# Block 0 of the gathered expert FFN: the weighted sum over rows of v as matmuls on PE, by token, in a PSUM bank that the recurrent mixer had

## The chip, the cores and the metric

One core of a Trainium2 chip runs one program. The metric is the time of one execution on the device in microseconds (us). An engine takes its instructions in the order of its own queue: PE is TensorE (PEld its weight loads), DVE is VectorE, ACT is ScalarE, POOL is GpSimd, and SP issues most of the DMAs.

## What is computed

A decoder block over 1,024 tokens of width 1,024: an RWKV-7 recurrent mixer and a differential attention side by side, merged by sigmoid gates, and then a PEER feed-forward. Of 16,384 experts each token chooses 128 (8 heads of 16); a row of `u_tab` gives each chosen expert its activation and a row of `v_tab`, weighted by it, is added up:

```
s = jnp.einsum('thcd,hcnd->thcn', q, sub_keys)
...
ids = (e1 * PK_NKEYS + e2).reshape(T, PK_HEADS * PK_TOPK)
gates = jax.nn.softmax(vals, axis=-1).reshape(T, PK_HEADS * PK_TOPK)
...
act = jnp.einsum('ced,cd->ce', u_tab[idc], xc)
act = jax.nn.gelu(act, approximate=False) * gc
return jnp.einsum('ce,ced->cd', act, v_tab[idc])
```

A final RMSNorm follows. All inputs and outputs are float32.

## The kernel before

The tokens go in two groups of 512 (`GROUPS`), and each group in blocks of 128 tokens. `mix` does a group's norm, input projections, four recurrent heads (`rwkv`), four attention heads (`attention`), the merge, the output projection (`w_out`) and the second norm; `pick` scores the keys. `choose` turns a block's scores into `ids` and `gate`. The four blocks of the first group go by **gathers** (`peer`): for each of the 128 choices j an indirect DMA from the POOL queue (`gather`) brings 128 rows of u, one for each token, into a tile `uv` of 128 x 1024 float32 (512 KB), and one DVE instruction multiplies it with the block's normed input `hb` and sums it into `act[:, j]` (L814). After the Gelu and the product with `gate` the same is done with v: DVE adds `v * act[:, j]` to `acc` (L821). All gathers share `NU` = 5 tiles `uv`. `finish` is the final norm and the store.

The four blocks of the second group go **dense** (`gates`, `ahead`, `dense`): all 128 stripes of 128 experts are computed by PE (`ua` is u against the tokens, `yk` and `yr` the weighted sums of v; six of the eight outputs are kept in PSUM over the whole loop, two are added to `accd` by DVE at L904).

`choose` of blocks 0 to 3 is called between the heads of the second group's mixer (`CHO`). The calls of `peer` stand last in the program, after `dense`. A planner orders each engine's queue: an instruction is put in when its inputs and a free buffer are there by the planner's own clock, the earlier in the program the more urgent. So the gathers and their DVE steps fill places that the planner found free in the second mixer, in `pick` and `gates`, and in `dense`.

PSUM has eight banks: two `zb` (projections, `q`, `ua`, `yr`), three `rb` (all that `rwkv` makes on PE), two `ab` and one `ob` (attention, transposes). The tag `ha` has two tiles of 128 x 1024, which hold `hb` and `acc` of the gathered blocks. `w_out` fills all eight banks at once (four token blocks by two column halves), and the additions to x (L668) come after the last matmul.

Names that the steps touch: `rbank` L62, `rwkv` L280 to L483 with its pairs of banks in `byfeat` (L421 to L430, read at L439, L442, L446, L450), `am` L331, `choose` L711, `gather` L790, `peer` L806, `dense` L861, the last loop L951.

Of the kernel before, what the change touches and what calls it, by code (L numbers as in the profile page):

```python
# [8 lines left out]
F32 = mybir.dt.float32  # L9
F32R = mybir.dt.float32r  # L10
BF = mybir.dt.bfloat16
I32 = mybir.dt.int32
U32 = mybir.dt.uint32
AF = mybir.ActivationFunctionType
OP = mybir.AluOpType
# [3 lines left out]
P = 128  # L19
D = 1024  # L20
T = 1024
# [8 lines left out]
NU = 5  # L30
ND = 4
NB = 5
NW = 3
# [14 lines left out]
def body(ctx: ExitStack, tc: tile.TileContext, ins, out, dbg=None):  # L48
# [13 lines left out]
    def rbank(name):  # L62
        return ps.tile([P, 512], F32, name=name, tag="rb", bufs=3)

# [179 lines left out]
    def mix(gi, t0, W):  # L244
# [409 lines left out]
        for a in range(TT):  # L654
            x1.append(t4("x1"))
            nc.sync.dma_start(x1[a], ins["x"][t0 + a * P:t0 + (a + 1) * P, :])
        banks = [f("xo") for f in (zbank, zbank, rbank, rbank, rbank, abank, abank, obank)[:2 * TT]]
        for k in range(8):
            w = [wsplit(ins["w_out"][k, i]) for i in range(2)]
            for a in range(TT):  # L660
                o = slice(a * P, (a + 1) * P)
                for i in range(2):
                    mm3(banks[2 * a + i], mh[k][:, o], ml[k][:, o], *w[i], k == 0, k == 7)
        for a in range(TT):
            rows = slice(t0 + a * P, t0 + (a + 1) * P)
            xs = [x1[a][:, c] for c in HALVES]
            for i in range(2):
                nc.vector.tensor_tensor(xs[i], xs[i], banks[2 * a + i], op=OP.add)  # L668
            nc.sync.dma_start(ins["x1s"][rows, :], x1[a])
            show("x1", x1[a], t0 // P + a)  # L670
            hn = normed(xs, nw)
            if t0 + a * P < T - ND * P:
                for i, c in enumerate(HALVES):
                    nc.sync.dma_start(ins["hfs"][rows, c], hn[i])
            to_cols(hn, a, fh, fl)
# [35 lines left out]
    def choose(v1, i1, bi, last):  # L711
# [75 lines left out]
        show("gate", gate, bi)  # L787
        return sl if last else (ids, gate)

# [15 lines left out]

    def peer(bi, ids, gate):  # L806

        rows = slice(bi * P, (bi + 1) * P)
        act = pp_.tile([P, P], F32, name="act", bufs=2)
        hb = pp_.tile([P, D], F32, name="hb", tag="ha", bufs=2)  # L810
        nc.sync.dma_start(hb, ins["hfs"][rows, :])
        for j in range(P):
            u = gather("u", ids, j)
            nc.vector.scalar_tensor_tensor(u, u, 1.0, hb, op0=OP.mult, op1=OP.mult, accum_out=act[:, j:j + 1])  # L814
        nc.scalar.activation(act, act, AF.Gelu)
        nc.vector.tensor_tensor(act, act, gate, op=OP.mult)
        acc = pp_.tile([P, D], F32, name="acc", tag="ha", bufs=2)
        nc.sync.dma_start(acc, ins["x1s"][rows, :])
        for j in range(P):
            v = gather("v", ids, j)  # L820
            nc.vector.scalar_tensor_tensor(acc, v, act[:, j:j + 1], acc, op0=OP.mult, op1=OP.add)  # L821
        finish(acc, rows, pp_, "uv", NU)

    def gates(sp, a, sl, eye8):
# [36 lines left out]
    def dense(t0, W, fh, fl):  # L861
# [7 lines left out]
        outs = [(a, 0) for a in range(TT)] + [(a, 1) for a in range(TT)][::-1]  # L869
        banks = (rbank, rbank, rbank, obank, abank, abank)  # L870
        kept = {o: f("yk") for o, f in zip(outs, banks)}
# [66 lines left out]
    if "nopeer" not in dbg:  # L938
        with tc.tile_pool(name="sp", bufs=1) as sp:
# [6 lines left out]
            for a, c in enumerate(late[o // P:]):  # L946
                gates(sp, a, choose(*c), eye8)
                ahead(sp, ND * P, fh, fl, range(a * NE // ND, (a + 1) * NE // ND))
            todo += [(c[2], *choose(*c)) for c in late[:o // P]]
        dense(t0 + o, ND * P, fh, fl)  # L950
        for t in todo:  # L951
            peer(*t)


def prepare(inputs):
# [31 lines left out]
    for b in (16, 32):  # L987
# [17 lines left out]

SCRATCH = {"x1s": (T, D), "hfs": (T, D), "k_s": (4, P, T), "v_s": (4, P, T),
           "y_s": (4, 8, P, 512), "g_s": (4, 16, P, 512),
# [20 lines left out]
```

## Time and profile before

| | us |
|---|---|
| median of 3 runs | 3537.24 |
| lowest and highest | 3536.96, 3545.42 |
| the profiled execution | 3524.41 |
| its span, first to last instruction | 3522.5 |

| engine | busy us | share of the span | instructions |
|---|---|---|---|
| PE | 3075.7 | 87% | 17382 |
| DVE | 2923.6 | 83% | 6546 |
| ACT | 1363.1 | 39% | 2506 |
| POOL | 1332.3 | 38% | 1036 |

The DMA engines are busy for most of the second half, and the mean rate is 255 GB/s. The span falls into stages that are best read apart: the first mixer and `pick` (0 to about 747 us, with the start of the second mixer in it), the second mixer to about 1466, `pick` to about 1600, `gates` and `ahead` to about 2015, `dense` to about 3476, and the end. The engine's busy shares in those stages, and in the heads of the mixers, are in the section of rows below.

### The profile page before, as it was taken

The page shows a single profiled execution, that of the slowest core. Times are in us where ns is not written, and L with a number is a line of the kernel's source. Part 1 is how long each engine was busy: PE and PEld are TensorE (multiplying, and loading weights), DVE is VectorE, ACT ScalarE, POOL GpSimd, SP SyncE. Part 2 cuts the span into 40 slices and gives each one's busy share as a digit, 9 for nine tenths or more (in the row PEclk, how much of TensorE's full clock was granted, in tenths as well). Part 3 has the DMA queues.
Part 4 walks back from the last instruction along what each step waited for, and adds up shares of the span by engine and source line. Part 5 has one row for each costly group of instructions (what it writes and reads, how often), then busy time and mean ns, then how long its engine had stood idle before and what let it go on. Part 6 is the DMA issues. An engine that isn't in the chain of part 4 may idle for free. (4 is left out here: it accounts for less than half of the span.)

```text
span 3522.5 us, 50906 instructions
## 1 busy us (share of the span) xinstructions
PE 3075.7 (87%) x17382; PEld 2399.4 (68%) x17382; DVE 2923.6 (83%) x6546; ACT 1363.1 (39%) x2506; POOL 1332.3 (38%) x1036
## 2 busy tenths in 40 slices
PE   6999998998778966798888589999999999899994
PEld 5777776776556654676666467777777777777773
DVE  4656558978888878999877689998999999899998
ACT  3444434443424421336989433222223232222321
POOL 0000000025543454411223336655655655556554
PEclk9999999989788987899988799999999999999997
DMA  4222444257675789854678989999999999999997
GB/s 129 76 75 72 121 162 155 83 165 239 217 255 178 253 293 311 289 183 136 208 215 279 323 314 342 353 349 341 348 343 351 348 350 354 348 344 357 340 336 270
DMA packets 407524, 898.68 MB, mean 255 GB/s; under 512 B 69024, under 2 KB 140000, under 8 KB 403168
## 3 DMA queue, kind: packets, MB, share of 16 engines
q0 software_dynamic: 147456, 536.94, 43.7%
q1 hardware_dynamic: 259808, 358.49, 30.2%
q8 instruction: 137, 2.24, 0.3%
q14 instruction: 123, 1.01, 0.1%
HBM read 829.22 MB, written 66.07 MB: 254 GB/s over the span
## 5 line engine op out<-in xcount | busy, mean ns | idle before, releaser
L792 POOL DMA_INDIRECT uv<-u,ids x512 | 663.8, 1296 | 1259.3 <-DVE uv L814 622.4
L792 POOL DMA_INDIRECT uv<-v,ids x512 | 667.4, 1304 | 534.3 <-DVE acc L821 379.8
L821 DVE SCALAR_TENSOR_TENSOR acc<-uv,act,acc 128x1024 f32<-128x1024 f32 x512 | 655.5, 1280 | 63.8 <-DMA uv<-v,ids 57.2
L814 DVE SCALAR_TENSOR_TENSOR uv<-uv,hb 128x1024 f32<-128x1024 f32 x512 | 615.6, 1218 | 74.1 <-DMA uv<-u,ids 73.5
L153 ACT ACTIVATE whi<-wraw 128x512 fp32r<-128x512 f32 x552 | 344.2, 629 | 702.2 <-PE z L169 205.5
L168 PE MATMUL ua<-fh,whi 128*128 128x512 f32 x1024 | 427.8, 418 | 95.2 <-DVE accd L904 71.8
L154 DVE TENSOR_TENSOR wlo<-wraw,whi 128x512 fp32r<-128x512 f32 x552 | 373.3, 684 | 140.4 <-ACT whi L153 129.8
L169 PE MATMUL ua<-fl,whi 128*128 128x512 f32 x1024 | 421.5, 412 | 0.0
L175 ACT ACTIVATE ah<-gw 128x512 fp32r<-128x512 f32 x128 | 80.8, 631 | 657.2 <-DVE gw L884 657.2
L179 PE MATMUL yk<-vh,ah 128*128 128x512 f32 x768 | 305.3, 398 | 21.8 <-DMA gw<-a_s 18.1
L168 PEld LDWEIGHTS ua<-fh,whi 128*128 128x128 f32 x1024 | 203.6, 199 | 160.8 <-DVE accd L904 91.8
L180 PE MATMUL yk<-vl,ah 128*128 128x512 f32 x768 | 305.2, 397 | 7.6 <-DVE vl L176 7.5
L181 PE MATMUL yk<-vh,al 128*128 128x512 f32 x768 | 304.9, 397 | 1.3 <-DVE al L176 1.3
L168 PE MATMUL z<-hh,whi 128*128 128x512 f32 x672 | 275.5, 411 | 1.0 <-ACT whi L153 1.0
L172 PE MATMUL z<-hh,wlo 128*128 128x512 f32 x672 | 274.5, 409 | 0.6 <-DVE wlo L154 0.6
L169 PE MATMUL z<-hl,whi 128*128 128x512 f32 x672 | 274.6, 409 | 0.0
L172 PE MATMUL ua<-fh,wlo 128*128 128x512 f32 x1024 | 264.7, 399 | 6.2 <-DVE wlo L154 6.2
L843 PE MATMUL gb<-oh,ohg 128*128 128x128 f32 x1024 | 227.5, 343 | 42.4 <-ACT ohg L842 41.9
L843 PEld LDWEIGHTS gb<-oh,ohg 128*128 128x128 f32 x1024 | 167.0, 210 | 105.7 <-ACT ohg L842 69.3
L169 PEld LDWEIGHTS ua<-fl,whi 128*128 128x128 f32 x1024 | 203.8, 199 | 43.7
L842 ACT ACTIVATE ohg<-ohb,sl 128x128 f32<-128x128 bf16 x512 | 230.1, 551 | 1.9 <-DVE ohb L837 1.9
L172 PEld LDWEIGHTS ua<-fh,wlo 128*128 128x128 f32 x1024 | 195.0, 191 | 49.9 <-DVE wlo L154 7.1
(320 smaller groups left out, 5672.3 us busy)
## 6 DMA issues: line engine op xcount, KB each, us to landing
wraw<-ut SPq DMA_DIRECT2D x256, 256.0 KB, 6.3
vraw<-v SPq DMA_DIRECT2D x256, 256.0 KB, 6.6
wraw<-w_in SPq DMA_DIRECT2D x168, 256.0 KB, 2.8
gd_s<-st SPq DMA_DIRECT2D x16, 2048.0 KB, 12.4
gt<-gd_s SPq DMA_DIRECT2D x32, 1024.0 KB, 9.2
wraw<-wq SPq DMA_DIRECT2D x64, 256.0 KB, 2.8
g_s<-sgo SPq DMA_DIRECT2D x32, 256.0 KB, 2.7
wraw<-proj SPq DMA_DIRECT2D x32, 256.0 KB, 4.2
```

Source lines behind the costliest of these rows:

```text
L153: nc.scalar.activation(hi, raw, AF.Copy)
L154: nc.vector.tensor_tensor(lo, raw, hi.bitcast(F32), op=OP.subtract)
L168: nc.tensor.matmul(o, hi, xh(k), start=(k == 0), stop=False)
L169: nc.tensor.matmul(o, hi, xl(k), start=False, stop=False)
L172: nc.tensor.matmul(o, lo, xh(k), start=False, stop=(k == n - 1))
L179: nc.tensor.matmul(o, ah, bh, start=first, stop=False)
L180: nc.tensor.matmul(o, ah, bl, start=False, stop=False)
L181: nc.tensor.matmul(o, al, bh, start=False, stop=last)
L792: nc.gpsimd.indirect_dma_start(out=t, out_offset=None, in_=ins[src], in_offset=bass.IndirectOffsetOnAxis(ap=ids[:, j:j + 1], axis=0))
L814: nc.vector.scalar_tensor_tensor(u, u, 1.0, hb, op0=OP.mult, op1=OP.mult, accum_out=act[:, j:j + 1])
L821: nc.vector.scalar_tensor_tensor(acc, v, act[:, j:j + 1], acc, op0=OP.mult, op1=OP.add)
L843: nc.tensor.matmul(b[:, k * P:(k + 1) * P], o3[:, k], o1[:, k], start=True, stop=True)
```

## The change

Block 0 alone (`VP = (0,)`) gets its sum over v from PE. `choose` also makes `idsT`, the block's ids with the choices over partitions and the tokens along the row. `values` makes `actT` by a transpose, and then takes one token at a time: a gather by `idsT[:, t]` brings the 128 rows of v that token t chose, and four matmuls (one for each 256 of the 1,024 columns) sum them over partitions. The stationary operand is 128 x 32 and zero outside the column of token i; 32 tokens accumulate in the same 32 partitions, and the four column chunks stand in the four groups of 32 partitions of one bank. ACT writes the 32 columns of `wa` anew for each 32 tokens and copies the bank out after each 64; eight small DMAs store it in `yv_s`, and at the end one load and one DVE addition bring it to `acc`. `values` stands under `high_priority`. `peer` of block 0 is called ahead of `dense`. The new bank `vb` takes one of the three `rb`; `dense` keeps an output in it. `w_out` runs in two passes of four banks, by column half, with the additions of a half after its pass. `NB` (tiles `ids` and `gate`) goes from 5 to 4.

```diff
--- before.py
+++ after.py
@@ -29,7 +29,8 @@
 N4 = 4
 NU = 5
 ND = 4
-NB = 5
+NB = 4
+VP = (0,)
 NW = 3
 NRAW = 4
 NVR = 6
@@ -60,7 +61,10 @@
         return ps.tile([P, 512], F32, name=name, tag="zb", bufs=2)
 
     def rbank(name):
-        return ps.tile([P, 512], F32, name=name, tag="rb", bufs=3)
+        return ps.tile([P, 512], F32, name=name, tag="rb", bufs=2)
+    def vbank(name):
+        return ps.tile([P, 512], F32, name=name, tag="vb", bufs=1)
 
     def abank(name):
         return ps.tile([P, 512], F32, name=name, tag="ab", bufs=2)
@@ -654,18 +658,19 @@
         for a in range(TT):
             x1.append(t4("x1"))
             nc.sync.dma_start(x1[a], ins["x"][t0 + a * P:t0 + (a + 1) * P, :])
-        banks = [f("xo") for f in (zbank, zbank, rbank, rbank, rbank, abank, abank, obank)[:2 * TT]]
-        for k in range(8):
-            w = [wsplit(ins["w_out"][k, i]) for i in range(2)]
+        for i, fs in enumerate(((zbank, zbank, rbank, rbank), (abank, abank, obank, zbank))):
+            banks = [f("xo") for f in fs[:TT]]
+            for k in range(8):
+                w = wsplit(ins["w_out"][k, i])
+                for a in range(TT):
+                    o = slice(a * P, (a + 1) * P)
+                    mm3(banks[a], mh[k][:, o], ml[k][:, o], *w, k == 0, k == 7)
             for a in range(TT):
-                o = slice(a * P, (a + 1) * P)
-                for i in range(2):
-                    mm3(banks[2 * a + i], mh[k][:, o], ml[k][:, o], *w[i], k == 0, k == 7)
+                xs = x1[a][:, HALVES[i]]
+                nc.vector.tensor_tensor(xs, xs, banks[a], op=OP.add)
         for a in range(TT):
             rows = slice(t0 + a * P, t0 + (a + 1) * P)
             xs = [x1[a][:, c] for c in HALVES]
-            for i in range(2):
-                nc.vector.tensor_tensor(xs[i], xs[i], banks[2 * a + i], op=OP.add)
             nc.sync.dma_start(ins["x1s"][rows, :], x1[a])
             show("x1", x1[a], t0 // P + a)
             hn = normed(xs, nw)
@@ -785,7 +790,17 @@
         nc.vector.scalar_tensor_tensor(ids, e[0], 128.0, e[1], op0=OP.mult, op1=OP.add)
         show("ids", ids, bi)
         show("gate", gate, bi)
-        return sl if last else (ids, gate)
+        if last:
+            return sl
+        if bi not in VP:
+            return ids, gate, None
+        nc.vector.scalar_tensor_tensor(pf, e[0], 128.0, e[1], op0=OP.mult, op1=OP.add)
+        b = abank("idT")[:, 0:P]
+        nc.tensor.transpose(b, pf, ident)
+        idsT = pp_.tile([P, P], I32, name="idsT", bufs=2)
+        nc.vector.tensor_copy(idsT, b)
+        return ids, gate, idsT
 
     def gather(src, ids, j):
         t = pp_.tile([P, D], F32, name="uv", bufs=NU)
@@ -803,7 +818,7 @@
         nc.vector.scalar_tensor_tensor(acc, acc, r[:, 0:1], fnw, op0=OP.mult, op1=OP.mult)
         nc.sync.dma_start(out[rows, :], acc)
 
-    def peer(bi, ids, gate):
+    def peer(bi, ids, gate, idsT):
 
         rows = slice(bi * P, (bi + 1) * P)
         act = pp_.tile([P, P], F32, name="act", bufs=2)
@@ -814,12 +829,52 @@
             nc.vector.scalar_tensor_tensor(u, u, 1.0, hb, op0=OP.mult, op1=OP.mult, accum_out=act[:, j:j + 1])
         nc.scalar.activation(act, act, AF.Gelu)
         nc.vector.tensor_tensor(act, act, gate, op=OP.mult)
-        acc = pp_.tile([P, D], F32, name="acc", tag="ha", bufs=2)
-        nc.sync.dma_start(acc, ins["x1s"][rows, :])
-        for j in range(P):
-            v = gather("v", ids, j)
-            nc.vector.scalar_tensor_tensor(acc, v, act[:, j:j + 1], acc, op0=OP.mult, op1=OP.add)
+        if idsT is None:
+            acc = pp_.tile([P, D], F32, name="acc", tag="ha", bufs=2)
+            nc.sync.dma_start(acc, ins["x1s"][rows, :])
+            for j in range(P):
+                v = gather("v", ids, j)
+                nc.vector.scalar_tensor_tensor(acc, v, act[:, j:j + 1], acc, op0=OP.mult, op1=OP.add)
+        else:
+            with tc.high_priority():
+                values(bi, act, idsT)
+            acc = pp_.tile([P, D], F32, name="acc", tag="ha", bufs=2)
+            nc.sync.dma_start(acc, ins["x1s"][rows, :])
+            y = pp_.tile([P, D], F32, name="uv", bufs=NU)
+            nc.sync.dma_start(y, ins["yv_s"][bi % 2])
+            nc.vector.tensor_tensor(acc, acc, y, op=OP.add)
         finish(acc, rows, pp_, "uv", NU)
+    def values(bi, act, idsT):
+        b = vbank("aT")[:, 0:P]
+        nc.tensor.transpose(b, act, ident)
+        actT = pp_.tile([P, P], F32, name="actT", bufs=1)
+        nc.scalar.activation(actT, b, AF.Copy)
+        wa = pp_.tile([P, D], F32, name="wa", tag="ha", bufs=2)
+        nc.gpsimd.memset(wa, 0.0)
+        for c in range(0, P, 32):
+            nc.scalar.activation(wa[:, 0:D:32], actT[:, c:c + 32], AF.Copy)
+            if c % 64 == 0:
+                b = vbank("yv")
+            o = slice(c % 64 * 8, c % 64 * 8 + 256)
+            for i in range(32):
+                v = gather("v", idsT, c + i)
+                for k in range(4):
+                    nc.tensor.matmul(b[32 * k:32 * k + 32, o], wa[:, 31 * i:31 * i + 32], v[:, 256 * k:256 * k + 256],
+                                     start=(i == 0), stop=(i == 31))
+            if c % 64:
+                t = pp_.tile([P, D], F32, name="uv", bufs=NU)
+                nc.scalar.activation(t[:, 0:512], b, AF.Copy)
+                for n in range(2):
+                    t0 = c - 32 + 32 * n
+                    for k in range(4):
+                        nc.sync.dma_start(ins["yv_s"][bi % 2, t0:t0 + 32, 256 * k:256 * k + 256],
+                                          t[32 * k:32 * k + 32, 256 * n:256 * n + 256])
 
     def gates(sp, a, sl, eye8):
 
@@ -867,7 +922,7 @@
             acc.append(t4("accd"))
             nc.sync.dma_start(acc[a], ins["x1s"][t0 + a * P:t0 + (a + 1) * P, :])
         outs = [(a, 0) for a in range(TT)] + [(a, 1) for a in range(TT)][::-1]
-        banks = (rbank, rbank, rbank, obank, abank, abank)
+        banks = (rbank, rbank, vbank, obank, abank, abank)
         kept = {o: f("yk") for o, f in zip(outs, banks)}
         moved = outs[len(banks):]
         gt = [None]
@@ -947,8 +1002,10 @@
                 gates(sp, a, choose(*c), eye8)
                 ahead(sp, ND * P, fh, fl, range(a * NE // ND, (a + 1) * NE // ND))
             todo += [(c[2], *choose(*c)) for c in late[:o // P]]
+        for t in todo[:len(VP)]:
+            peer(*t)
         dense(t0 + o, ND * P, fh, fl)
-        for t in todo:
+        for t in todo[len(VP):]:
             peer(*t)
 
 
@@ -1003,7 +1060,7 @@
     return a
 
 
-SCRATCH = {"x1s": (T, D), "hfs": (T, D), "k_s": (4, P, T), "v_s": (4, P, T),
+SCRATCH = {"x1s": (T, D), "yv_s": (2, P, D), "hfs": (T, D), "k_s": (4, P, T), "v_s": (4, P, T),
            "y_s": (4, 8, P, 512), "g_s": (4, 16, P, 512),
            "gd_s": (P // CE, P, 512, CE), "a_s": (NE, P, 512),
            "m_s": (2, 2, 8 * CHB), "z_s": (2, 2, 8 * CHB)}
```

## Rows read from the trace of the kernel before

**Rows 1.** Busy time by stage (a view of windows): the stretch, its length, then for PE, PEld, DVE, ACT and POOL the busy us and the count of instructions, the mean granted clock of PE, the DMA share and GB/s. The stretches are: the first heads of the second mixer, its last stretch, `gates` and `ahead`, `dense` after its start, the end.

```profile
747.00:1137.00 390.00, 320.87 (x2584) 242.84 (x2586) 328.80 (x994) 145.70 (x242) 186.55 (x136) 0.84 0.70 227
...
1232.00:1468.00 236.00, 162.43 (x1211) 128.25 (x1203) 197.46 (x312) 57.65 (x107) 117.33 (x96) 0.83 0.88 306
...
1600.00:2015.00 415.00, 325.63 (x1426) 242.79 (x1424) 331.13 (x856) 328.01 (x715) 104.99 (x87) 0.87 0.73 231
...
2113.00:3476.00 1363.00, 1288.87 (x5411) 1029.06 (x5410) 1271.80 (x1687) 390.28 (x674) 808.98 (x618) 0.98 0.95 345
3476.00:3522.50 46.50, 3.52 (x16) 2.48 (x14) 34.91 (x94) 5.64 (x10) 12.85 (x11) 0.56 0.74 253
```

**Rows 2.** When things happen (the view of single lines: durations in ns, then the first and last start in us): the product of act and gate of the four gathered blocks, the v steps, the last matmuls of `dense`, the additions of `w_out`.

```profile
L816 DVE TENSOR_TENSOR act<-act,gate x4: 274/284/292, 1137.5 to 3229.5; 128x128 f32<-128x128 f32 x4
...
L821 DVE SCALAR_TENSOR_TENSOR acc<-uv,act,acc x512: 1232/1283/1331, 1138.7 to 3505.0; 128x1024 f32<-128x1024 f32 x171
...
L181 PE MATMUL yk<-vh,al x768: 390/394/628, 2016.7 to 3476.3; 128*128 128x512 f32 x192
...
L668 DVE TENSOR_TENSOR x<-x,xo x16: 673/679/681, 540.6 to 1463.8; 128x512 f32<-128x512 f32 x16
```

**Rows 3.** The DVE steps on v alone (line L821) in stretches of 40 us: four in and after the second mixer's fourth head, one near block 0's end, and the program's last: length, DVE busy us and count, granted clock, DMA share, GB/s.

```profile
1240.00:1280.00 40.00, 20.36 (x16) 0.96 0.79 282
1280.00:1320.00 40.00, 26.91 (x21) 0.66 0.92 313
1320.00:1360.00 40.00, 26.91 (x21) 0.60 0.87 287
1360.00:1400.00 40.00, 12.79 (x10) 0.85 0.95 344
...
1440.00:1480.00 40.00, 14.12 (x11) 0.80 0.84 307
...
3480.00:3520.00 40.00, 17.90 (x14) 0.52 0.75 255
```

**Rows 4.** Heads of the mixers (windows, columns as in Rows 1): the first group's fourth head from the end of the one before, the second group's third and fourth head, then from the scan L296 to the last product L481 of the fourth head, first and second group.

```profile
350.90:445.60 94.70, 94.42 (x936) 70.67 (x935) 53.54 (x169) 46.58 (x81) 0.11 (x1) 1.00 0.41 122
...
1037.30:1188.90 151.60, 121.13 (x1065) 92.57 (x1066) 129.47 (x359) 58.93 (x96) 70.91 (x51) 0.86 0.68 223
1188.90:1351.30 162.40, 105.94 (x1000) 81.61 (x999) 134.25 (x259) 49.04 (x83) 79.76 (x63) 0.80 0.80 275
...
369.00:445.60 76.60, 76.32 (x852) 57.32 (x851) 45.10 (x135) 37.71 (x66) 0.11 (x1) 1.00 0.41 121
1218.90:1351.30 132.40, 79.53 (x897) 63.50 (x896) 110.19 (x193) 35.62 (x66) 75.92 (x61) 0.77 0.85 288
```

**Rows 5.** The gathered blocks: from the view of instructions by line and shape the two DVE steps (busy us, mean ns of one, idle time before them and what ended it), then the page's row of the landing of a v gather (median us).

```profile
L821 DVE SCALAR_TENSOR_TENSOR acc<-uv,act,acc 128x1024 f32<-128x1024 f32 x512 | 655.5, 1280 | 63.8 <-DMA uv<-v,ids 57.2
L814 DVE SCALAR_TENSOR_TENSOR uv<-uv,hb 128x1024 f32<-128x1024 f32 x512 | 615.6, 1218 | 74.1 <-DMA uv<-u,ids 73.5
...
uv<-v,ids POOLq DMA_INDIRECT x512, 7.0
```

**Rows 6.** Steps on u (line L814; each is counted with its read of the accumulator, so two for a step), in stretches of 40 us: the first of block 1, and its last.

```profile
1440.00:1480.00 40.00, 1.21 (x2) 0.80 0.84 307
1480.00:1520.00 40.00, 12.70 (x23) 0.90 0.73 243
...
2080.00:2120.00 40.00, 2.44 (x4) 0.96 0.87 303
```

**Rows 7.** PE at full clock (timeline: start, us to the end of the last, form, count). A change of tiling: matmuls of the whole array, two with 64 rows and 256 columns moved (one float32 product is two such instructions), the whole array again. Then four instructions of 128 columns on the whole array, and 32 of 128 columns on 64 x 64 tiles.

```profile
200.83 0.39 PE L169 MATMUL z<-hl,whi 128*128 128x512 f32 x1
201.06 0.39 PE L172 MATMUL z<-hh,wlo 128*128 128x512 f32 x1
201.38 0.70 PE L527 MATMUL sc<-kTn,qT 64*128 64x256 f32 x2
202.01 0.50 PE L168 MATMUL z<-hh,whi 128*128 128x512 f32 x1
202.34 0.39 PE L169 MATMUL z<-hl,whi 128*128 128x512 f32 x1
...
1213.69 0.66 PE L241 MATMUL hb<-ident,rb 128*128 128x128 f32 x4
...
1231.30 1.10 PE L331 MATMUL am<-KR,bT 64*64 64x128 f32 x32
```

**Rows 8.** Waits in 1137 to 1468 us (who <- for whom, us in total, times, longest), and the window in which PE waited longest (columns as in Rows 1).

```profile
DVE acc L821 <- DMA uv<-v,ids: 20.7, 23, 2.5
PE xtr L391 <- DMA XT<-z_s: 21.9, 2, 19.7
...
1280.00:1300.00 20.00, 3.21 (x36) 2.65 (x38) 15.03 (x18) 0.60 (x1) 13.97 (x11) 0.50 1.04 366
```

**Rows 9.** POOL's gathers of block 0 in a stretch where DVE did little else (timeline: start, us taken, idle before and its end): the first and the last of seven in a row.

```profile
1284.12 1.86 POOL L792 DMA_INDIRECT uv<-v,ids  x1 [0.75 <-DVE pr L375]
...
1294.47 1.32 POOL L792 DMA_INDIRECT uv<-v,ids  x1 [0.30 <-issue]
```

**Rows 10.** Reads of the mixer's banks, and a copy of a whole bank by ACT (instructions by line and shape: busy us, mean ns | idle before).

```profile
L442 DVE TENSOR_TENSOR Qm<-Qp,G 128x256 f32<-128x256 f32 x16 | 6.2, 417 | 4.5 <-PE Qp L429 4.5
...
L883 ACT ACTIVATE gw<-ua 128x512 f32<-128x512 f32 x112 | 67.0, 598 | 118.3 <-PE ua L172 118.2
```

## The prediction

> **What bounds the kernel now.** I read the windows by stage first, since the shares over the whole span mix stages with different limits. In `dense`, from 2113 to 3476 us, PE is busy 1289 of 1363 us and DVE 1272 [rows 1]: both are nearly full, and PE's last matmul at 3476 is followed by an end of 46 us in which DVE still works off v steps and the final norms [rows 1, 2, 3]. In the second mixer neither is full (PE 321 of 390 us, then 162 of 236) [rows 1]. There the heads tell more: a head of the first group takes 95 us with PE busy for all of it; the third and fourth heads of the second take 152 and 162 us with PE busy 121 and 106, at a granted clock of 0.86 and 0.80 [rows 4]. The recurrent chain of the fourth head, scan to last product, lasts 132.4 us against 76.6 in the first group, and DVE is busy 110 us in it against 45 [rows 4]; some 74 us of that, from 1240 to 1360 us, are v steps of block 0 [rows 3]. So DVE steps of 1.28 us stand in its queue between the short steps of a chain for which PE waits. The next stages hang on the mixer's end, so each us there moves the end of `dense`.
>
> **The DVE work removed.** 128 steps of 1.28 us [rows 5], 164 us, between 1138 and about 1475 us [rows 2, 6]. Not all of it was on the path. The fourth head's chain is 55.8 us longer than the first group's; attention over twice the keys and `choose` also lengthen it, so between 0 and 55.8 us I take half, -28; of the third head only 52 us lie behind 1137 us, and I take -5.
>
> **The PE work added.** For each token four products with 32 stationary columns, 256 moved, in the four column groups, each of two instructions. One product of that length with both changes of tiling is in the trace: from the z matmul at 201.06 to that at 202.34 us are 1.28 us, of which two z matmuls are 0.46 (they follow each other by 0.23), so 0.82 us [rows 7]. Whether four lie side by side the trace shows only for 64 x 64 tiles: 32 instructions of 128 columns take 1.10 us there, 0.034 each, against 0.66 for four on the whole array, 0.165 each [rows 7]. That is four at a time, so I take 0.82 us a token, 105 us for 128. If they go one after another, each further one costs two steps of 0.32 (two such instructions take 0.70 to the end of the second; one of 512 columns takes 0.39, so I take 0.38 for the last one [rows 7]): 0.82 + 3 x 0.64 = 2.74 us, 351 us in all. PE idles 87 us in the two heads and some 20 behind them [rows 1, 4], so most of the 105 has room, but its places are not free: in the fourth head alone some 94 tokens (its 162 us at the pace of 1.73 us below) want 77 us where 56 are idle. I put +15 on the path for it.
>
> The Trainium skill's page "TensorE: Matmul & The Clock Gate", section "Measured speedup vs the span model", gives three column tiles of 32 a speedup of only 2.38, by which four would be about 3.2 by proportion. As an estimate from that, a token's instructions would stretch by about a quarter, some 13 us over the 128; the 64 x 64 rows show more, and no run here shows column groups alone.
>
> **The wait added.** PE now waits for gathers, and behind a waiting matmul stand all projections and the recurrent chain in its queue. DVE's wait for v gathers of block 0 was 20.7 us in all [rows 8], 0.16 a gather. The pace of gathers is (1294.47 - 1284.12) / 6 = 1.73 us [rows 9], with a landing of 7.0 [rows 5] and five tiles. From below the wait is 0, where PE is late anyway; from above 1.73 - 0.82 = 0.9 us a token, 116 us. I take DVE's, and half of it on the path: +10. The four writings of `wa` and two copies of a bank (0.60 us for a whole one [rows 10]) stop PE's tokens for about 4 us in all, inside the same slack. Sixteen stores of 32 KB and one load pass through SP ahead of some weight loads; the transposes for `idsT` and `actT`, the memset on POOL and the final addition on DVE (bound by one v step, 1.28 us) are single instructions. I take +1 for all of these, 0 to 5.
>
> **The third bank.** In `byfeat` a call fills two banks; the third let the next call start before both were read, and a read is 0.417 us [rows 10]. Four calls at up to 2 x 0.417 are 3.3 us a head, and with `am` and the transposes I bound it at 6, so 0 to 48 us for eight heads. In the first group PE is full (94.4 of 94.7 us [rows 4]) and has projections to put there: +4 for four heads, as long as that cover lasts, else 24. In the second group +10.
>
> **w_out in halves** lets four additions of 0.68 us [rows 2] run beside the second pass, in each group: -3 together. Fewer tiles `ids` and `gate` cost nothing: blocks 0 to 3 hold one each, and the next is wanted long after block 0's product with `gate` at 1137 us [rows 2] has freed one. The call ahead of `dense` moves nothing either, since block 0's steps are over before block 1's begin at about 1475 us already; `dense` finds its bank free unless block 0 lasted to 2015 us.
>
> The mixers together: -28 - 5 + 15 + 10 + 1 + 4 + 10 - 3 = **+4 us**.
>
> **What comes later.** The last gather of block 0 is issued about 1137 + 128 x 1.73 = 1358 us; block 1 needs the tile `ha` that `wa` frees then, and starts near 1375 instead of 1475, where its first steps now are [rows 6]. At the 10 to 11 steps in 40 us that DVE managed there [rows 3], it is some 26 steps ahead when `pick` begins, and I let it keep them. In `dense` a step takes 1363 / 618 = 2.2 us [rows 1], so the gathered blocks end 57 us earlier: from 3505 us [rows 2] to about 3448, before PE's last matmul. PE's 5411 matmuls at 0.23 us are 1245 us, so 118 of the 1363 are lost, 0.19 for each of the 618 steps [rows 1, 7]: 26 fewer give **-5**. In the end 17.9 us of v steps [rows 3] leave DVE's queue ahead of the norms: **-18**.
>
> **Sum.** +4 - 5 - 18 = -19 us on a span of 3522.5. That profiled execution took 3524.4 us, 0.4% under the median of 3537.2; the same share of the median gives 3518 us.
>
> **Rivals.** *PE waits where DVE did* (slower). Place: the third and fourth heads, 1137 to 1351 us. The matmuls by token are urgent, so the planner puts them where it believes a gather is landed; if gathers come slower than its belief, PE stands still while the chain waits behind. At 0.5 us a token, midway between 0.16 and 0.9, PE would want 227 + 105 + 64 = 396 us in two heads that have 314 [rows 4]: 82 us over, where I counted 25, so 3518 + 57 = 3575. It decides from about 0.3 us a token, where the 19 us are gone. For it speaks that the planner gives these matmuls no slack; against it, that the wait at 1138 to 1475 us was small.
>
> *The whole excess goes.* The fourth head falls to the first group's 76.6 us and PE's waits fit in its idle time: -28 more, and ten us in the third head, 3480. The DVE share of the chain speaks for it, the longer attention against it.
>
> *The bank is dear.* If the first group's cover is thinner than it looks, 34 of the 48 us more than I counted remain: 3552.
>
> *The clock falls.* In the 20 us around PE's longest wait, 19.7 us for a DMA, the granted clock was 0.50, the 1.2 GHz level [rows 8]. If waits for gathers kept PE there for half of both heads, its 227 us (at about 0.83) would be some 300 at 0.63, 75 more: 3518 + 75 = 3593. Against it: a wait lasts at most 0.9 us, and 0.82 us of work stands between two. The Trainium skill names this pattern, a DMA wait between every two matmuls, as the bad loop that takes the clock down (page "TensorE: Matmul & The Clock Gate", section "Loop structure matters more than you think"); the trace agrees for one long wait and shows none of this pattern.
>
> *The change doesn't do what it says*: the four column groups run one after another. PE then wants 351 us and not 105, more than all idle time in the second mixer: 3518 + 246 = 3764.
>
> **How the numbers follow.** Forecast 0.45, the whole excess 0.15, PE waits 0.20, bank 0.10, clock 0.05, one after another 0.05. A measurement of this kernel tells about 0.3% from no change, 10.6 us. Of the forecast, whose unknown mixer terms spread it over 3495 to 3540, I count 0.31 as faster, 0.12 as the same, 0.02 as slower; the bank splits 0.03 and 0.07. Faster 0.46, same 0.15, slower 0.39. The range 3460 to 3600 leaves out the last rival, half of the clock, and the outer parts of the waits and of the excess, about 0.16. The likeliest case's own range is 3495 to 3540.
>
> **What would show it.** Right: no DVE v steps before block 1; a scan-to-product chain of the fourth head near 100 us; matmuls by token about 0.8 us from first to next form, starts 1.7 us apart; block 1's first u step near 1375 us; v steps over before PE's last matmul, and an end near 28 us. Wrong: PE idle before these matmuls for a gather by more than 0.3 us on average; heads of the first group longer than 95 us; block 1 no earlier than now; four matmuls of a token starting one after another.

## The result, and the profile after

The changed kernel takes 3582.3 us (median of five runs, 3570.4 to 3586.8 but for one of 5986.6 that the comparison leaves out) against 3537.39: ratio 1.0111 [1.009, 1.0133] (the 95% interval), slower by 1.1%, some 39 us. The forecast was 3518 us. The profiled execution took 3586.76 us, its span is 3585.0; before's had 3522.5. Of these 62.5 us some 20 are the choice of executions (before's profile lies 13 below its median, this one 7 above the median of the other four, 3579.7), so a second profile of the changed kernel (`e12_again`, span 3564.9) stands beside it below.

Windows of the kernel after (stretch, length, busy us and count of PE, PEld, DVE, ACT, POOL, granted clock, DMA share, GB/s): the first group's first and fourth head; the fourth head of the second group, its chain from scan to last product, from there to the last addition of `w_out`; most of the tokens' stretch in two; `dense`; the end.

```profile
91.00:180.20 89.20, 87.21 (x862) 64.46 (x862) 48.44 (x157) 37.14 (x67) 0.11 (x1) 0.92 0.22 59
...
377.80:476.30 98.50, 98.02 (x937) 72.03 (x936) 53.56 (x169) 46.73 (x81) 0.99 (x2) 1.00 0.38 116
...
1222.80:1380.80 158.00, 147.92 (x1507) 80.01 (x1506) 59.51 (x177) 46.20 (x77) 71.25 (x73) 0.92 0.85 284
1255.20:1380.80 125.60, 115.52 (x1291) 63.75 (x1286) 43.01 (x134) 35.67 (x63) 54.14 (x56) 0.90 0.82 266
1380.80:1534.10 153.30, 140.45 (x727) 101.73 (x725) 98.30 (x182) 42.82 (x74) 57.03 (x54) 1.00 0.93 336
1161.00:1223.00 62.00, 59.64 (x923) 38.31 (x922) 23.47 (x124) 16.15 (x29) 31.75 (x34) 1.00 0.84 283
1223.00:1285.70 62.70, 62.61 (x492) 31.98 (x492) 33.79 (x88) 25.73 (x42) 31.55 (x32) 1.00 0.94 327
...
2180.00:3550.00 1370.00, 1291.64 (x5412) 1031.57 (x5411) 1262.58 (x1691) 393.39 (x679) 789.62 (x601) 0.98 0.94 340
3550.00:3585.00 35.00, 13.99 (x60) 10.92 (x59) 20.62 (x69) 6.35 (x11) 0.00 (x0) 0.76 0.34 121
```

Read against [rows 4], the fourth head's chain lasts 125.6 us where it lasted 132.4, though DVE is busy only 43 us in it and not 110: what left DVE's queue came back as PE time (115.5 us busy, before 79.5). The granted clock is 0.90 there and was 0.77. The last stretch of the mixer takes 153 us, before 112.5.

When things happen in the kernel after (durations in ns, first and last start): additions of `w_out`, u steps, v steps, the additions to `accd`, the last `dense` matmuls, the tokens' matmuls, and POOL's gathers for them.

```profile
L670 DVE TENSOR_TENSOR x<-x,xo x16: 679/681/685, 550.8 to 1534.1; 128x512 f32<-128x512 f32 x16
...
L829 DVE SCALAR_TENSOR_TENSOR uv<-uv,hb x512: 1168/1219/1297, 788.2 to 3243.6; 128x1024 f32<-128x1024 f32 x171
...
L837 DVE SCALAR_TENSOR_TENSOR acc<-uv,act,acc x384: 1267/1284/1320, 2056.1 to 3528.0; 128x1024 f32<-128x1024 f32 x192
...
L959 DVE TENSOR_TENSOR accd<-accd,yr x128: 667/679/698, 2112.7 to 3564.0; 128x512 f32<-128x512 f32 x128
...
L868 PE MATMUL yv<-uv,wa x1024: 378/402/637, 1161.3 to 1420.7; 128*32 128x256 f32 x171
...
L807 POOL DMA_INDIRECT uv<-v,idsT x128: 932/936/1637, 1142.2 to 1411.7; - x128
```

The mixer ends at 1534.1 where it ended at 1463.8 [rows 2]; v steps end 36 us ahead of the last addition to `accd`, where before they ended 22 behind it (3505.0 [rows 2] against 3482.8).

PE in the fourth head of the kernel after (timeline, as in Rows 7), three tokens between other work:

```profile
1299.27 0.40 PE L176 MATMUL z<-hh,wlo 128*128 128x512 f32 x1
1299.60 0.64 PE L868 MATMUL yv<-uv,wa 128*32 128x256 f32 x8
1300.17 1.38 PE L565 MATMUL pT<-dg,sc 128*128 128x128 f32 x10
1301.48 0.64 PE L868 MATMUL yv<-uv,wa 128*32 128x256 f32 x8
1302.05 1.38 PE L565 MATMUL pT<-dg,sc 128*128 128x128 f32 x10
1303.36 0.64 PE L868 MATMUL yv<-uv,wa 128*32 128x256 f32 x8
```

A token's eight instructions hold PE for 0.57 us until the next form starts, and are entered 0.33 us after a z matmul that is else followed after 0.23; with as much again behind them (as in [rows 7]) that is 0.77 us, 99 us for 128. They come every 1.9 us, and between them PE has hardly a gap (122.3 of 124.7 us busy from 1161 to 1285.7).

Waits of the kernel after in 1161 to 1421 us (who <- for whom, us, times, longest):

```profile
POOL uv L807 <- PE yv L868: 116.9, 87, 11.5
...
PEld yv L868 <- DMA uv<-v,idsT: 3.7, 9, 0.7
```

PE's weight loads waited 3.7 us for gathers; POOL waited 116.9 for PE to free a tile. So it is the gathers that run at PE's pace.

What the pushed work is: PE's groups in the tail of the mixer after, from the last product to the last addition (busy us, mean ns | idle before).

```profile
L176 PE MATMUL z<-hh,wlo 128*128 128x512 f32 x39 | 16.1, 412 | 0.0
L173 PE MATMUL z<-hl,whi 128*128 128x512 f32 x38 | 15.9, 418 | 0.0
L172 PE MATMUL z<-hh,whi 128*128 128x512 f32 x38 | 15.5, 409 | 1.2 <-ACT sgo L600 1.2
L868 PE MATMUL yv<-uv,wa 128*32 128x256 f32 x168 | 13.4, 391 | 0.4 <-issue 0.2
```

Before, no input projection and no token stands in that tail (1351.3 to 1463.8 us): there are only the merge's and `w_out`'s matmuls. Here 47.5 us of projections were still to do, beside 13.4 us of tokens.

### The profile page after: what moved, and what is told of

Its sections match the earlier page's. It is cut to its first block, busy times and chain, and to the rows that moved or that the text cites. A ratio compares the mean times of both kernels' runs of the same rounds, so it can differ in the third digit from the quotient of the medians.

```text
span 3585.0 us, 52823 instructions
## 1 busy us (share of the span) xinstructions
PE 3197.1 (89%) x18408; PEld 2436.2 (68%) x18408; DVE 2787.5 (78%) x6421; ACT 1368.1 (38%) x2513; POOL 1292.3 (36%) x1037
## 5 line engine op out<-in xcount | busy, mean ns | idle before, releaser
L807 POOL DMA_INDIRECT uv<-v,ids x384 | 505.1, 1315 | 449.2 <-DVE acc L837 358.9
L837 DVE SCALAR_TENSOR_TENSOR acc<-uv,act,acc 128x1024 f32<-128x1024 f32 x384 | 492.1, 1282 | 47.7 <-DMA uv<-v,ids 41.8
```

What stands on the lines that cost most here:

```text
L807: nc.gpsimd.indirect_dma_start(out=t, out_offset=None, in_=ins[src], in_offset=bass.IndirectOffsetOnAxis(ap=ids[:, j:j + 1], axis=0))
```

## The experiments

Three theories stood against each other. **PE's work**: the tokens' 99 us have no room where they are put, and cost nearly what they take. **The bank**: the recurrent mixer pays for the bank it lost. **The wait**: PE, or the chain behind it, waits for gathers. The table puts all profiles side by side: the last addition of the first mixer; from there to the last product of the second group's fourth head; from there to the mixer's last addition (us; read from the lines of these additions and products).

| kernel | banks `rb` | first mixer's end | to the last product | to the mixer's end | ratio of times |
|---|---|---|---|---|---|
| before | 3 | 545.2 | 806.1 | 112.5 | 1 |
| e3_halves | 3 | 543.8 | 821.5 | 112.5 | 0.9991 [0.9973, 1.0009] |
| e1_bank | 2 | 576.8 | 830.4 | 117.3 | 1.0061 [1.004, 1.0082] |
| e2_novp | 2 | 578.3 | 829.3 | 113.0 | 1.0067 [1.0042, 1.0092] |
| e5_noprio | 2 | 572.3 | 731.6 | 105.7 | 1.046 [1.0427, 1.0493] |
| e4_back | 3, one shared | 549.2 | 731.4 | 142.8 | 1.0121 [1.0067, 1.0175] |
| e9_half | 2 | 567.2 | 776.5 | 150.2 | 1.0058 [1.0038, 1.0078] |
| after | 2 | 575.0 | 805.9 | 153.2 | 1.0111 [1.009, 1.0133] |
| e12_again | 2 | 576.4 | 789.7 | 150.9 | 1.0130 [1.0102, 1.0157] |
| e8_double | 2 | 572.0 | 860.1 | 152.3 | 1.0378 [1.0338, 1.0417] |
| e7_later | 3, one shared | 544.2 | 827.0 | 103.9 | 1.0077 [1.0047, 1.0107] |
| e10_inter | 2 | 565.7 | 725.7 | 101.2 | 1.0388 [1.0365, 1.0412] |
| e11_inter_prio | 2 | 564.9 | 733.5 | 101.2 | 1.0269 [1.0244, 1.0293] |

Two profiles of one kernel (after, e12_again) differ by 16 us in the fourth column: less than that it can't tell. The runs were made on several chips, on which the kernel before takes 3516 to 3539 us (medians); each ratio is taken on one chip, the profiles in the other columns are not.

**The parts of the edit.** e1_bank is the kernel before with one bank `rb` taken and used only where all eight are:

```diff
-        return ps.tile([P, 512], F32, name=name, tag="rb", bufs=3)
+        return ps.tile([P, 512], F32, name=name, tag="rb", bufs=2)
...
+        return ps.tile([P, 512], F32, name=name, tag="vb", bufs=1)
```

> The kernel before with one bank taken from the mixer and nothing else (it stands in for the third in the output projection and in the dense loop). Bank theory: the heads of the first group go from 90 to 95 us to 98 to 101, its last addition of the output projection comes near 575 us instead of 545, and the whole is 25 to 45 us slower than before, 3562 to 3582. Rival, the two passes of the output projection or another order of the planner: the first mixer ends at 545 as before, the whole within 10 us of before.

e2_novp is the changed kernel with all sums on DVE again:

```diff
-VP = (0,)
+VP = ()
```

> The changed kernel with no block on PE (VP empty): bank, halves and tile counts as in the change, block 0 summed over v by DVE as before. Bank theory: as the run with the bank alone, 25 to 45 us over before. Theory that PE's own work in the second mixer costs: its end loses the some 40 us that the change adds between the last recurrent product and the last addition of the output projection (153 us in the change, 112 before), so 112 to 120 us here. If only the work on PE were to blame, the whole is within 10 us of before.

e3_halves is the kernel before with the change's loop of `w_out` alone:

```diff
-        banks = [f("xo") for f in (zbank, zbank, rbank, rbank, rbank, abank, abank, obank)[:2 * TT]]
...
+        for i, fs in enumerate(((zbank, zbank, rbank, rbank), (abank, abank, obank, zbank))):
+            banks = [f("xo") for f in fs[:TT]]
```

> The kernel before with the output projection in two passes alone, three banks in the mixer. Bank theory and PE theory: 0 to 5 us faster than before, the first mixer ends at 540 to 545. Rival, the passes cost (a bank that is waited for between them, or another order): 10 to 40 us slower, with the last addition of the first group near 560 to 575.

The bank alone costs 0.61%, some 22 us (25 to 45 were expected), and what else is in e2_novp adds nothing that can be told (0.67%). `w_out` in halves can't be told from nothing. Windows show where the bank costs. First e1_bank: the four heads of the first group, then a stretch in its first head.

```profile
91.00:179.00 88.00, 86.01 (x858) 63.77 (x859) 48.10 (x155) 36.37 (x66) 0.11 (x1) 0.92 0.22 59
179.00:278.50 99.50, 96.53 (x902) 71.55 (x901) 53.33 (x174) 42.40 (x74) 0.11 (x1) 0.91 0.23 66
278.50:379.90 101.40, 99.43 (x928) 74.91 (x927) 54.97 (x176) 43.17 (x76) 0.11 (x1) 0.95 0.25 73
379.90:478.50 98.60, 98.13 (x937) 72.12 (x936) 53.67 (x169) 46.75 (x81) 0.11 (x1) 1.00 0.38 116
...
99.00:103.00 4.00, 2.29 (x10) 1.19 (x9) 3.51 (x12) 1.89 (x3) 0.00 (x0) 0.88 0.32 100
103.00:107.00 4.00, 4.00 (x20) 2.07 (x18) 2.09 (x4) 0.00 (x0) 0.00 (x0) 0.50 0.00 0
107.00:111.00 4.00, 4.00 (x42) 3.34 (x42) 2.27 (x7) 0.73 (x4) 0.00 (x0) 0.50 0.16 37
111.00:115.00 4.00, 4.00 (x24) 3.37 (x21) 1.58 (x6) 0.84 (x4) 0.00 (x0) 0.50 0.51 115
```

The same of the kernel before: its first three heads, and the stretch of the same work.

```profile
91.00:167.50 76.50, 75.37 (x850) 57.10 (x849) 47.05 (x155) 35.63 (x66) 0.11 (x1) 1.00 0.23 62
167.50:257.20 89.70, 86.84 (x906) 65.70 (x905) 53.57 (x175) 42.20 (x74) 0.11 (x1) 1.00 0.26 76
257.20:350.90 93.70, 91.72 (x928) 69.70 (x928) 54.70 (x177) 42.42 (x76) 0.12 (x1) 1.00 0.28 79
...
99.00:103.00 4.00, 3.49 (x48) 1.98 (x48) 3.97 (x14) 1.63 (x3) 0.00 (x0) 1.00 0.28 68
103.00:107.00 4.00, 3.67 (x44) 3.07 (x41) 3.44 (x8) 1.04 (x2) 0.00 (x0) 1.00 0.21 53
```

And e1_bank's timeline (with the idle time before an instruction and its end):

```profile
100.34 0.70 PE L530 MATMUL sc<-kTn,qT 64*128 64x256 f32 x2 [0.39 <-DVE mx L532]
102.36 2.05 PE L320 MATMUL bb<-av,blk 128*128 128x512 f32 x2 [1.32 <-DVE kz L272]
104.33 1.97 PE L334 MATMUL am<-KR,bT 64*64 64x128 f32 x16
```

The same two products in the kernel before:

```profile
100.45 1.10 PE L317 MATMUL bb<-av,blk 128*128 128x512 f32 x2
101.48 1.10 PE L331 MATMUL am<-KR,bT 64*64 64x128 f32 x32
```

With a bank fewer PE comes to the product `bb` before its input is ready, is busy 2.29 of 4 us, and then the granted clock is 0.50 (the 1.2 GHz level) for some 12 us. The two instructions of `bb` take 2.05 us there and 1.10 in the kernel before, where the same stretch has 3.49 of 4 busy and keeps 1.00. The pattern comes again at 199 us (2.97 of 4) and 303 us (2.30 of 4) in e1_bank. From 91 us to the end of the fourth head, the four profiles with three banks last 355 to 360 us at a clock of 0.99 to 1.00, the nine with two 376 to 389 at 0.95 to 0.99. Length times clock is an estimate of what is left without the clock: 367 to 371 with two banks against 354 to 355. So by this estimate some 14 us come from the order of work and its waits, and 5 to 21 from the clock. Why the clock falls after these short gaps in some heads and not in others isn't settled by these runs.

The rows of `am` show a piece of the first part. It fills two banks at once, and its 64 x 64 products start by fours in the kernel before (thirty-two in 1.10 us). In e1_bank only sixteen, one bank's worth, are issued at first: they start by twos and take 1.97 us, with half as many side by side and at half the clock. In the four heads 128 of the 256 instructions of `am` start by fours with three banks, and 16 with two. How much of the 14 us this makes isn't separated here.

**The tokens without urgency.** e5_noprio is the changed kernel without `high_priority`:

```diff
-            with tc.high_priority():
-                values(bi, act, idsT)
+            values(bi, act, idsT)
```

> The changed kernel without the urgency (values at its own place in the program, behind pick, gates and ahead), its own bank kept, two for the mixer. Theory that PE's urgent work by token pushes the second mixer's end: the end loses 30 to 60 us (last product of the second group to last addition of the output projection 153 us in the change, about 110 here), since PE then takes tokens only where the mixer leaves it idle; the whole 15 to 40 us faster than the change, 3545 to 3565. Rival, where the work stands makes no difference since PE is full anyway: within 10 us of the change, 3573 to 3592.

Expected were 15 to 40 us less than the change; it is the worst of all, and tells most. Its tokens and steps on v (lines):

```profile
L867 PE MATMUL yv<-uv,wa x1024: 379/402/637, 1222.3 to 2002.2; 128*32 128x256 f32 x171
...
L837 DVE SCALAR_TENSOR_TENSOR acc<-uv,act,acc x384: 1265/1284/1335, 2318.4 to 3670.1; 128x1024 f32<-128x1024 f32 x192
...
L958 DVE TENSOR_TENSOR accd<-accd,yr x128: 668/680/705, 1974.5 to 3453.2; 128x512 f32<-128x512 f32 x128
```

Of 1024 matmuls only 38 run before its last product at 1304 us, so its mixer has block 0's v steps neither on DVE nor on PE. It ends at 1409.6, 54 us earlier than before's, and `dense` starts 59 earlier. But the tokens drag on to 2002 and hold the five tiles `uv`; no gather of another block is made before 2001.9 us, and the gathered blocks end at 3670, 217 us after `dense`.

**The bank given back.** e4_back lets the tokens' bank be one of three `rb`:

```diff
-        return ps.tile([P, 512], F32, name=name, tag="rb", bufs=2)
+        return ps.tile([P, 512], F32, name=name, tag="rb", bufs=3)
...
-        return ps.tile([P, 512], F32, name=name, tag="vb", bufs=1)
+        return rbank(name)
```

> The changed kernel with three banks for the mixer again, the one for v being one of the three, taken while block 0 is summed. Bank theory: the first mixer ends at 545 again instead of 575, the whole is 25 to 35 us faster than the change, 3545 to 3555. PE theory: the 40 us between the last recurrent product of the second group and its last addition stay, so it does not get below before's 3537. If the bank were not the cause, it stays at 3575 to 3585.

The first mixer is back at 549 us. The tokens start only at 1350, since the shared bank comes after the recurrent heads. Its fourth head from scan to last product (window), and POOL's wait:

```profile
1204.00:1280.50 76.50, 73.06 (x886) 55.90 (x886) 43.12 (x136) 33.01 (x62) 0.00 (x0) 0.98 0.25 73
```
```profile
POOL uv L807 <- PE yv L868: 319.7, 104, 211.5
```

76.5 us, the first group's 76.6 [rows 4]: the 55.8 us more went with DVE's v steps and their gathers, and none was the longer attention. (Steps and gathers aren't parted here: the DMA share in that chain is 0.25, before 0.85.) PE is busy for 73.1 of the 76.5 us, so a chain that DVE no longer holds up leaves PE next to no idle time. The mixer ends 40 us earlier than before's, but for 211.5 us no gather was made, and the gathered blocks end at 3560, behind `dense` at 3487. So the whole is no faster than the change (1.0121 beside 1.0111), where 25 to 35 us less were expected.

**The amount of PE work.** e8_double makes each token's matmuls twice, e9_half makes those of every second token alone:

```diff
+                for n in range(2):
...
+                                         start=(i == 0 and n == 0), stop=(i == 31 and n == 1))
```
```diff
+                if i % 2:
+                    continue
```

> The changed kernel with the matmuls by token issued twice (block 0's sum over v comes out doubled); gathers, bank and DVE work unchanged. Theory PE work: the second mixer's end moves by nearly all of the added 128 x 0.5 us, 45 to 65 us, and the whole by 40 to 65, to 3620 to 3650. Rival, the gathers set the pace of the tokens and PE has room between them: under 15 us.

> The changed kernel with matmuls for every second token alone (the sums of block 0's other tokens are left out); all 128 gathers stay. Theory PE work: 64 x 0.77 us less, the second mixer's end 30 to 50 us earlier, the whole 25 to 50 us faster than the change, 3530 to 3557. Rival, the gathers set the pace: within 10 us of the change.

A token of e8_double and the next form (timeline):

```profile
1301.58 1.07 PE L869 MATMUL yv<-uv,wa 128*32 128x256 f32 x16
1302.58 0.49 PE L172 MATMUL z<-hh,whi 128*128 128x512 f32 x1
```

In e8_double 16 instructions in a row take 1.00 us to the next form (eight took 0.57), so it adds 128 x 0.43 = 55 us; the second mixer is 53 us longer than the changed kernel's (72 than e12_again's). e9_half takes out 64 x 0.77 = 49 us and is 32 shorter (14 against e12_again). These two ran on one chip. From e9_half to e8_double the second mixer grows by 86 us for 104 us more of PE work, and the whole by 103 (medians 3538.1 and 3641.3), with all gathers made in both: that speaks for PE's work and against the wait. With half of the tokens' matmuls gone the time comes down to what the bank alone costs (1.0058 beside 1.0061), and no lower.

PE's work isn't quite all, though. From e5_noprio, on the same chip and with next to no tokens in its mixer, to e9_half the second mixer grows by 89 us for 49 us of PE work. The other 40 come with something else that the tokens bring: their gathers (the mixer's DMA share is 0.70 in place of 0.52), or the 24 u steps of block 1 that DVE then has in the mixer's tail. Which isn't shown, and the two profiles of the changed kernel differ by 18 us in this sum.

**Other places for the tokens.** e7_later keeps three banks and puts the u steps of block 1 ahead of block 0's v, whose tokens then fall without urgency into `pick` and `gates`; e10_inter takes a token and a u step of block 1 in turn, e11_inter_prio the same with urgent matmuls. Their core:

```diff
-        for t in todo[:len(VP)]:
-            peer(*t)
+        acts = [first(*t) for t in todo[:2]]
+        second(acts[0], *todo[0])
```
```diff
+                ustep(*nxt, other[1], c + i)
...
+                with tc.high_priority():
```

> A version that might beat both: three banks for the mixer; block 0's and block 1's u first, on DVE as before, then block 0's v on PE without urgency, in a bank of the recurrent mixer that is then idle, in pick, gates and ahead; then block 1's v. Theory: the mixers stay as before (last addition of the output projection near 1464 to 1478 us), PE's tokens take idle time of gates (about 90 us there), the gathered blocks end earlier than before while dense starts within 15 us of before: 3505 to 3535. Rival, PE's tokens push pick and gates as they pushed the mixer: 20 to 70 us slower than before.

> A version that might beat both: as the changed kernel, not urgent, with block 1's u on DVE and block 0's v on PE taken in turn, so that the five gather tiles serve both engines. Without urgency the mixer, pick and gates ended some 60 us earlier than before but the gathered blocks 165 us later, since block 0's v held the five tiles alone until 2002 us. Theory: what is gathered before dense is block 0 and block 1's u, as before, but with 128 fewer DVE steps, so dense starts 10 to 50 us earlier than before and the blocks end no later than before: 3480 to 3520 where before takes 3537, a ratio of 0.985 to 0.995. Rival, PE's late places stall the tiles for both engines: gathered blocks end 50 us or more after before, ratio over 1.01.

> The same in turn, with the matmuls by token urgent. Theory: gathers no longer wait for PE, block 1's u ends with block 0's v; PE's tokens stand at one in two gathers, some 3.5 us apart, so they push the second mixer less than in the change; second mixer's end between before and the change, the gathered blocks earlier than before: ratio 0.99 to 1.01. Rival, the DVE steps of u and PE's tokens both delay the chain: ratio over 1.015.

e12_again is the changed kernel once more, on the chip of the last two.

> The changed kernel once more, to stand on the same chip as the two versions above: a ratio of 1.009 to 1.013.

It takes 3567.71 us beside 3522.62 for the kernel before there, 1.0130 [1.0102, 1.0157]: the changed kernel's loss is the same within the intervals.

e7_later keeps the mixers as before, as expected, but takes 1.0077 [1.0047, 1.0107] and not less than before; its tokens run from 1479 to 2069 us. e10_inter: 1.0388 [1.0365, 1.0412]; POOL's waits in it, and the tokens of e11_inter_prio:

```profile
POOL uv L807 <- PE yv L879: 554.2, 69, 239.9
...
L880 PE MATMUL yv<-uv,wa x1024: 379/403/637, 1404.0 to 2127.6; 128*32 128x256 f32 x171
```

e11_inter_prio: 1.0269 [1.0244, 1.0293]. In both, a free tile goes in turn to a token that PE isn't ready for, and the u gathers behind it stand, for some 240 us at the longest. Neither has a token in its mixer, not even with urgent matmuls (the first is at 1397 and 1404 us, behind the mixer's last addition), so e11_inter_prio doesn't test what it was meant to, tokens spread thinner over the mixer. No place was found where the tokens pay: all six versions with them (after, e4_back, e5_noprio, e7_later, e10_inter, e11_inter_prio) are slower than before, and the kernel before, or e3_halves, remains the fastest.

## Why the prediction was wrong

It forecast -19 us and the runs give about +39. The step that failed first is "**The PE work added**", its "+15 on the path". The amount was right (105 us forecast, 99 measured), but "most of the 105 has room" was wrong. From e5_noprio to the changed kernel, the tokens in the mixer add 74 us up to the last product and 48 behind it, 122 together (103 with e12_again): as much as PE's work, and more. PE's idle time in the two heads of [rows 4] was not free room: most of it stood there because DVE's steps held up the chain. Once DVE was relieved the chain needed PE in just those places, as the fourth head of e4_back and the full PE of 1161 to 1285 us show, and what the urgent tokens displaced, 47.5 us of projections among it, came back behind the last product.

"**The DVE work removed**" (-33) was under-sized for the same reason. From before to e4_back it is -75 us up to the last product, with -56 in the fourth head's chain where the sum took half. From e2_novp to e5_noprio, both with two banks, the second mixer is 105 us shorter; in e10_inter and e11_inter_prio, which have neither v steps nor tokens in it either, 115 and 108. The rival *the whole excess goes* was right on this side. Relief and work together, e2_novp to the two profiles of the changed kernel, are +17 and -2 us in the second mixer, where the sum had -18, or -8 with the wait: two large errors that nearly cancel. By the medians the trade as a whole costs 0.4 to 0.6% beyond the bank (1.0111 and 1.0130 beside 1.0067), 16 to 22 us.

"**The third bank**" was the other failed step: +4 in the first group, "as long as that cover lasts". All kernels with two banks end the first mixer at 565 to 578 us, those with three at 544 to 549. The cover held PE busy, but neither at the clock nor with as many products side by side: by the estimate above some 14 us are order and 5 to 21 the 1.2 GHz level after short gaps. e1_bank's 22 us alone are more than the whole forecast gain. In the second mixer its +10 can't be told: +23 with DVE's steps in place (e2_novp), 0 without (e4_back, with three, and e5_noprio, with two, reach the last product after 731.4 and 731.6 us).

*PE waits where DVE did* came nearest in time (3575) for a wrong reason: PE waited 3.7 us in all, not 0.5 for each token, and POOL waits for PE. The "+10" of the sum for that wait is nearly nothing, too. *The clock falls* was right that a short wait can bring the 1.2 GHz level, but it was in the first mixer, from the bank; in the tokens' stretch the clock rose. *The change doesn't do what it says* is out: 0.57 us for eight instructions. *The bank is dear* holds by itself (22 us); with the 16 to 22 of the trade it makes the loss of 39 to 45.

Behind the mixer: block 1's first u step came at 1453 us (1437 in e12_again) and not 1375, since the tokens took PE's pace, 2.1 us a gather ((1411.7 - 1142.2) / 127), and freed `wa` at 1421. The "-5" in `dense` was 0: from first to last addition to `accd` it takes 1449 us before, 1451 and 1447 in the two profiles of the changed kernel, and 1447 to 1451 in e1_bank, e2_novp, e3_halves and e4_back. The **-18** at the end came out (21 us from the last addition to `accd` to the end, before 40), but by luck. The v steps did not end 57 us earlier: they ended 23 later than before (3528.0; 3507.8 in e12_again), and are over in time only because `dense` ends 61 to 81 later. The kernels with a bank fewer and every v step on DVE have the same short end, 20 us in e1_bank and 21 in e2_novp, whose v steps and additions to `accd` are:

```profile
L837 DVE SCALAR_TENSOR_TENSOR acc<-uv,act,acc x512: 1234/1283/1345, 1152.8 to 3541.0; 128x1024 f32<-128x1024 f32 x171
...
L959 DVE TENSOR_TENSOR accd<-accd,yr x128: 667/678/700, 2106.9 to 3556.4; 128x512 f32<-128x512 f32 x128
```

So none of the 23 us that the sum took off behind the mixer is shown to be the tokens' gain.

The terms in the profiles of the changed kernel, after and e12_again: first mixer +30, +31; second mixer +41, +22; between mixer and `dense` +9, +10; `dense` +2, -2; end -19, -19: +63 and +42 us (the spans: +62.5, +42.4).

## What to carry to other kernels

Idle time of an engine next to a chain that another engine holds up isn't room for new work: relieve the chain in the estimate first, and see how much of the idle time is left. Work that is marked urgent on a full engine costs about all that it takes, even if what it displaces only shows up a stage later; and work that is not urgent, but holds buffers of a shared ring, stops everyone behind it. A buffer taken from a stage with a full engine is worth an experiment by itself, since short gaps can cost the clock, and products that fill two buffers at once may no longer run side by side. And a term that comes out right in size is still to be looked for in the runs without the change that it was put down to.

## What was not expected of the hardware

Products with 32 stationary columns in four column groups of one bank do run side by side: 1,024 moved columns in float32, eight instructions, hold PE for 0.57 us between changes of tiling, and sixteen for 1.00.

A stretch of 4 us with PE busy for 2.3 was followed by some 12 us at a granted clock of 0.50 with PE busy all the time (e1_bank, 103 to 115 us). The two instructions of `bb` at its edge took 2.05 us; before, at full clock, 1.10.
